# Order of long and short matmuls inside the products of an encoder layer's seven-product units

## The chip, the cores and the metric

The kernel runs on one core of a Trainium2 chip. The metric is device time in microseconds (us) of one execution. A core has a matrix engine (TensorE, here PE; the loading of its stationary operand is shown apart as PEld), a vector engine (VectorE, DVE), a scalar engine (ScalarE, ACT), a general one (GpSimd, POOL) and SyncE (SP), which here issues most of the DMA transfers. Each engine runs its own list of instructions in order, and semaphores tie the lists together. Working memory is SBUF; PE adds up its results in eight banks of PSUM.

## The reference

One encoder layer on 512 tokens of width 2048, in float32. Cut to what matters here:

```python
h = rmsnorm(x, attn_norm_w)
proj = h @ w_in                      # 2048 -> 6176 columns
attn_out = mixture_of_dilations(...) # 16 heads of 64, three windows
gla_out = ...                        # gated linear attention, both directions
x = x + concat(attn_out, gla_out) @ w_out
h = rmsnorm(x, ffn_norm_w)
x = x + (silu(h @ w_gate) * (h @ w_up)) @ w_down   # hidden width 5632
return rmsnorm(x, final_norm_w)
```

The matrix products with `w_in`, `w_gate`, `w_up` and `w_down` are most of the work.

## The kernel before, in words

Large products are computed in float32 accuracy from operands that are each split in a rounded part (`hi`) and the rest (`lo`). A product of two such numbers takes hi times hi, hi times lo and lo times hi; lo times lo is left out.

Part of the products with `w_in`, `w_gate` and `w_up` goes by a scheme that computes a two by two block product with seven block products instead of eight (Strassen's scheme in Winograd's form). The class `Units` does this. One *unit* is a block of 256 weight columns against all 512 tokens and the whole depth of 2048. It needs seven sums of weight blocks; each sum is a tile of 128 partitions by `NP` = 8 pieces of 128 columns. The sums of activations are made once and kept in `self.xs[q][name]`, one tile for each piece `q`, which holds 256 columns of hi next to 256 columns of lo.

One of the seven products (`products`) is sixteen matmuls into one PSUM bank. Eight **long** ones (512 moving columns, line 1669) multiply the eight pieces of the weights' hi tile with the activations' hi and lo together: hi times hi goes to the first half of the bank, hi times lo to the second. Eight **short** ones (256 moving columns, line 1672) multiply the eight pieces of the weights' lo tile with the activations' hi, and add to the first half. Every matmul loads another stationary operand of 128 by 128.

The tiles for product i are made in `lead(i)`, which is called two products ahead (`AHEAD` = 2): `cast` on ACT rounds the sum to hi (line 1631), `sub` on DVE subtracts it from the sum to get lo (line 1637), and `add` on DVE makes the next sum (line 1606) from weight blocks that SyncE loads (line 1599). After a product, `evac_` reads its bank with ACT and DVE. Where a later product of the unit adds to a result that is known already, `seat` first runs one long matmul on a fresh bank (line 1655) whose result is overwritten by that known value; it stands between two products.

Each engine's order is that of the program text. The hi and lo tiles come from one pool of `b` tiles (`s4`); `put(hi, lo)` gives them back after the product, and whoever writes such a tile next waits for its last reader.

Other streams of matmuls that the profile shows: lines 356 to 358 and 2118 to 2120 are long matmuls only (plain products and the one with `w_down`), lines 1768 to 1770 are short ones only (a unit in smaller pieces), and lines 731 and 732 are eight short ones in the attention, between transposes (line 707) and long ones.

Of the kernel before, what the change touches and what calls it, by code (L numbers as in the profile page):

```python
# [116 lines left out]
def put(*slots):  # L117
    for s in slots:
        if s.home is not None:
            s.home.free.append(s.i)  # L120


def layer(nc, tc, x, attn_norm_w, w_in, rel_table, gw_f, gb_f, gw_b, gb_b, gla_norm_w, w_out,
# [5 lines left out]
    mm = pe.matmul  # L129

    with tc.manual_schedule(), \
# [1190 lines left out]
        NP = KT // 2  # L1322
# [253 lines left out]
        class Units:  # L1576
# [82 lines left out]
            def products(self, i):  # L1659
                u, n = self.steps[i]  # L1660
                hi, lo = self.both.pop(i)
                k = "XVYXWZW"[n]
                new = n < 2
                if new:
                    b = self.banks[u, k] = ps.get()
                    ps.full.add(b.i)
                o = self.banks[u, k].t
                for q in range(NP):
                    mm(o.rearrange("p (s t) -> p s t", s=2), hi.t[:, q], self.xs[q][self.ORDER[n]],  # L1669
                       start=new and q == 0, stop=False, skip_group_check=True)  # L1670
                for q in range(NP):
                    mm(o[:, 0:256], lo.t[:, q], self.xs[q][self.ORDER[n]][:, 0], start=False, stop=q == NP - 1,  # L1672
                       skip_group_check=True)
                put(hi, lo)
                self.late_.append(i)

# [576 lines left out]
        def finish():  # L2253
# [43 lines left out]
            def last(ys):  # L2297
# [6 lines left out]
                for h in range(2):  # L2304
                    cols = slice(h * 256, (h + 1) * 256)
                    b = seeded.popleft()
                    products(b, t, c, cols)
                    dve.scalar_tensor_tensor(x_[:, cols], b.t[:, cols], rstd2[:, t:t + 1], x_[:, cols],
                                             op0=OP.mult, op1=OP.add)
                    put(b)  # L2310
                    if h == 0:
                        act.activation(junk.t[:, cols], x_[:, cols], AF.Square, accum_out=ss1[:, 3:4])
                        act.activation(ss1[:, 8:13], ss1[:, 0:5], AF.Copy, scale=1.0 / D, accum_out=total)
                        dve.tensor_tensor(ys[c].t[:, cols], x_[:, cols], wf[c].t[:, cols], op=OP.mult)
                        continue
                    dve.tensor_tensor_reduce(junk.t[:, cols], x_[:, cols], x_[:, cols], 1.0 / D, 0.0,
                                             op0=OP.mult, op1=OP.add, accum_out=sq)
                    act.activation(q, sq, AF.Ln, bias=total)
                    act.activation(r, q, AF.Exp, scale=-0.5)
                    dve.tensor_tensor(m, sq, total, op=OP.add)  # L2320
                    dve.tensor_tensor(ys[c].t[:, cols], x_[:, cols], wf[c].t[:, cols], op=OP.mult)
# [8 lines left out]
            def run():  # L2330
                ys = {t: [] for t in range(4)}
                behind = []

                def rest(t, c, b, y):
                    residual(c, t, b)
                    squares(c, t, x1[c], ss2 if t < 3 else ss1[:, 0:4], 0 if t == 3 else 4 * t)
                    if t == 3:
                        dve.tensor_tensor(y.t, x1[c][t].t, wf[c].t, op=OP.mult)
                    if c == 3:
                        later(t, ys[t])  # L2340
                        put(*ys[t], *(x1[c][t] for c in range(4)))

                for t, c in ORDER:
                    seed()
                    y = s2.get()
                    ys[t].append(y)
                    if (t, c) == (3, 3):
                        last(ys[t])
                        break
                    b = seeded.popleft()  # L2350
                    products(b, t, c, slice(0, 512))
                    behind.append((t, c, b, y))
                    while len(behind) > (t < 2):
                        rest(*behind.pop(0))
# [45 lines left out]
```

## Time and profile before

| what | value |
|---|---|
| three runs, median (lowest to highest) | 2131.49 us (2129.62 to 2131.94) |
| the profiled execution's own time | 2129.54 us |
| its span in the profile | 2127.3 us |
| granted TensorE clock, mean | 0.999 |
| long matmuls of the units (line 1669) | 3,248 |
| short matmuls of the units (line 1672) | 3,248 |
| seven-product units' products | 406 |

The profile comes from one execution. Its span runs from the first instruction of the program to the end of the last; the time of that execution is 2.2 us longer. "Busy" adds the recorded durations of an engine's instructions. In the timeline a row is a run of equal instructions: its first start, the time until its end, engine, line, operation, the tile written and those read, and how many. Matmuls overlap, and their ends are modelled, so a row's second number is longer than the time until the next row begins. In a view of one line, the durations of the instructions stand as lowest, median and highest in ns.

### The profile page before, as it was taken

The page shows a single profiled execution, that of the slowest core. Times are in us where ns is not written, and L with a number is a line of the kernel's source. Part 1 is how long each engine was busy: PE and PEld are TensorE (multiplying, and loading weights), DVE is VectorE, ACT ScalarE, POOL GpSimd, SP SyncE. Part 2 cuts the span into 40 slices and gives each one's busy share as a digit, 9 for nine tenths or more (in the row PEclk, how much of TensorE's full clock was granted, in tenths as well). Part 3 has the DMA queues.
Part 4 walks back from the last instruction along what each step waited for, and adds up shares of the span by engine and source line. Part 5 has one row for each costly group of instructions (what it writes and reads, how often), then busy time and mean ns, then how long its engine had stood idle before and what let it go on. Part 6 is the DMA issues. An engine that isn't in the chain of part 4 may idle for free.

```text
span 2127.3 us, 30896 instructions
## 1 busy us (share of the span) xinstructions
PE 2117.0 (100%) x11370; PEld 1822.8 (86%) x11370; DVE 1756.2 (83%) x2381; ACT 1281.3 (60%) x2152; POOL 205.5 (10%) x384
## 2 busy tenths in 40 slices
PE   9999999999999999999999999999999999999998
PEld 7888888888888889988888888888888888888886
DVE  6688888778877568888888999999999798876696
ACT  8454444468776556555555555555555477877774
POOL 0000000123222000000000011011011201111100
PEclk9999999999999999999999999999999999999999
DMA  6644544656664233444443445455455788975662
GB/s 206 177 130 129 139 139 135 181 156 194 195 177 122 98 119 100 139 123 125 120 128 113 151 145 172 139 165 158 142 166 157 276 292 297 332 243 184 228 218 80
DMA packets 342405, 355.65 MB, mean 167 GB/s; under 512 B 16686, under 2 KB 261918, under 8 KB 342255
## 3 DMA queue, kind: packets, MB, share of 16 engines
q1 hardware_dynamic: 310638, 251.78, 38.8%
q0 software_dynamic: 31296, 101.38, 13.6%
q8 instruction: 90, 1.47, 0.3%
q14 instruction: 61, 0.49, 0.1%
q10 hardware_dynamic: 320, 0.53, 0.1%
HBM read 289.57 MB, written 64.06 MB: 166 GB/s over the span
## 4 chain that ended last, share of the span: by engine, by line
PE 96%; DVE 2%; ACT 1%; issue 1%; DVEq 0%; ACTq 0%
PE ps L1669 35%; PE ps L1672 18%; PE ps L2120 6%; PE ps L2118 6%; PE ps L2119 6%; PE ps L358 5%; PE ps L356 5%; PE ps L357 5%; PE ps L707 1%; PE ps L732 1%; PE ps L651 1%; PE ps L731 1%; PE ps L652 1%; PE ps L1769 1%; PE ps L1768 1%
## 5 line engine op out<-in xcount | busy, mean ns | idle before, releaser
L1637 DVE TENSOR_TENSOR b<-b,b 128x1024 fp32r<-128x1024 f32 x406 | 495.7, 1221 | 73.4 <-ACT b L1631 71.3
L1631 ACT CAST b<-b 128x1024 fp32r<-128x1024 f32 x406 | 421.1, 1052 | 21.4 <-DMA b<-in_w_in_dram 15.1
L1669 PE MATMUL ps<-a,b 128*128 128x512 f32 x1656 | 424.5, 392 | 0.0
L1669 PE MATMUL ps<-b,b 128*128 128x512 f32 x1592 | 421.0, 393 | 0.0
L1669 PEld LDWEIGHTS ps<-a,b 128*128 128x128 f32 x1656 | 304.3, 188 | 62.6 <-ACT ps L1703 0.2
L1669 PEld LDWEIGHTS ps<-b,b 128*128 128x128 f32 x1592 | 280.2, 189 | 42.4
L1606 DVE TENSOR_TENSOR b<-b,b 128x1024 f32<-128x1024 f32 x232 | 282.6, 1218 | 12.8 <-DMA b<-in_w_in_dram 12.8
L1672 PEld LDWEIGHTS ps<-b,b 128*128 128x128 f32 x1592 | 232.6, 190 | 23.4
L1672 PE MATMUL ps<-b,b 128*128 128x256 f32 x1592 | 242.9, 282 | 0.0
L1672 PE MATMUL ps<-a,b 128*128 128x256 f32 x1656 | 242.6, 283 | 0.0
L1672 PEld LDWEIGHTS ps<-a,b 128*128 128x128 f32 x1656 | 224.7, 191 | 8.3
L2086 DVE TENSOR_TENSOR b<-b,b 128x1024 fp32r<-128x1024 f32 x140 | 170.7, 1221 | 69.4 <-ACT b L2078 66.3
L1697 ACT COPY b<-ps 128x256 f32<-128x256 f32 x126 | 46.9, 372 | 243.0 <-PE ps L1672 241.6
L2078 ACT CAST b<-b 128x1024 fp32r<-128x1024 f32 x140 | 146.4, 1049 | 17.0 <-DVE b L2066 7.2
L2118 PE MATMUL ps<-b,b 128*128 128x512 f32 x368 | 143.2, 389 | 0.0
L2119 PE MATMUL ps<-b,b 128*128 128x512 f32 x368 | 143.2, 389 | 0.0
L2120 PE MATMUL ps<-b,b 128*128 128x512 f32 x368 | 143.2, 389 | 0.0
L356 PE MATMUL ps<-b,b 128*128 128x512 f32 x256 | 104.7, 409 | 0.0
L358 PE MATMUL ps<-b,b 128*128 128x512 f32 x256 | 100.3, 392 | 0.1
L357 PE MATMUL ps<-b,b 128*128 128x512 f32 x256 | 100.0, 391 | 0.0
L2119 PEld LDWEIGHTS ps<-b,b 128*128 128x128 f32 x368 | 69.1, 188 | 14.4
L2120 PEld LDWEIGHTS ps<-b,b 128*128 128x128 f32 x368 | 69.1, 188 | 14.3
(307 smaller groups left out, 3610.7 us busy)
## 6 DMA issues: line engine op xcount, KB each, us to landing
b<-in_w_in_dram SPq DMA_DIRECT2D x94, 512.0 KB, 5.3
b<-in_w_gate_dram SPq DMA_DIRECT2D x88, 512.0 KB, 6.2
b<-in_w_up_dram SPq DMA_DIRECT2D x88, 512.0 KB, 4.5
b<-in_w_down_dram SPq DMA_DIRECT2D x88, 512.0 KB, 5.4
b<-gx POOLq DMA_DIRECT2D x46, 512.0 KB, 6.8
gx<-a POOLq DMA_DIRECT2D x84, 256.0 KB, 4.4
b<-in_w_out_dram SPq DMA_DIRECT2D x32, 512.0 KB, 4.3
a<-gx POOLq DMA_DIRECT2D x48, 256.0 KB, 6.0
```

The source lines that it names most:

```text
L356: mm(o, xh.t[:, c], wh.t[:, w], start=first and not on, stop=False, skip_group_check=on)
L357: mm(o, xh.t[:, c], wl.t[:, w], start=False, stop=False, skip_group_check=on)
L358: mm(o, xl.t[:, c], wh.t[:, w], start=False, stop=last, skip_group_check=on)
L1606: tt = lambda o, x_, y_: dve.tensor_tensor(o.t, x_.t, y_.t, op=OP.add)
L1631: act.copy(hi.t, home[key].t)
L1637: dve.tensor_tensor(lo.t, home[key].t, hi.f, op=OP.subtract)
L1669: mm(o.rearrange("p (s t) -> p s t", s=2), hi.t[:, q], self.xs[q][self.ORDER[n]], start=new and q == 0, stop=False, skip_group_check=True)
L1672: mm(o[:, 0:256], lo.t[:, q], self.xs[q][self.ORDER[n]][:, 0], start=False, stop=q == NP - 1, skip_group_check=True)
L2086: dve.tensor_tensor(lo.t, s.t, hi.f, op=OP.subtract)
L2118: mm(o, xh[:, t], wh, start=not ch and first and j == 0, stop=False, skip_group_check=True)
L2119: mm(o, xh[:, t], wl, start=False, stop=False, skip_group_check=True)
L2120: mm(o, xl[:, t], wh, start=False, stop=last and j == 1, skip_group_check=True)
```

## The change

Inside a product the sixteen matmuls are put in another order. Before, all eight long ones ran, then all eight short ones. Now the eight pieces go by pairs: for two pieces the long matmuls, then for the same two pieces the short ones, and so on four times. Each matmul has the operands and the bank that it had. The first of a product still opens the bank (`start`), and the last short one still closes it (`stop`).

```diff
-                for q in range(NP):
-                    mm(o.rearrange("p (s t) -> p s t", s=2), hi.t[:, q], self.xs[q][self.ORDER[n]],
-                       start=new and q == 0, stop=False, skip_group_check=True)
-                for q in range(NP):
-                    mm(o[:, 0:256], lo.t[:, q], self.xs[q][self.ORDER[n]][:, 0], start=False, stop=q == NP - 1,
-                       skip_group_check=True)
+                for p in range(0, NP, 2):
+                    for q in (p, p + 1):
+                        mm(o.rearrange("p (s t) -> p s t", s=2), hi.t[:, q], self.xs[q][self.ORDER[n]],
+                           start=new and q == 0, stop=False, skip_group_check=True)
+                    for q in (p, p + 1):
+                        mm(o[:, 0:256], lo.t[:, q], self.xs[q][self.ORDER[n]][:, 0], start=False, stop=q == NP - 1,
+                           skip_group_check=True)
```

The first place is on PE, in the third product of the kernel's first unit (the one that starts at 110.18 us in the trace before). A row gives the line, the tile written, the two read (activations, then the weights' hi or lo tile) and what the matmul waits for. Before (`b_109` is hi, `b_110` is lo):

```order
L1669 MATMUL ps_34_1105<-a_15_309,b_109_1084 128x512 [waits Activation_49]
L1669 MATMUL ps_34_1105<-a_23_382,b_109_1084 128x512
L1669 MATMUL ps_34_1105<-a_33_487,b_109_1084 128x512
L1669 MATMUL ps_34_1105<-a_41_608,b_109_1084 128x512
L1669 MATMUL ps_34_1105<-a_46_698,b_109_1084 128x512
L1669 MATMUL ps_34_1105<-a_50_799,b_109_1084 128x512
L1669 MATMUL ps_34_1105<-a_54_865,b_109_1084 128x512
L1669 MATMUL ps_34_1105<-a_58_929,b_109_1084 128x512
L1672 MATMUL ps_34_1105<-a_15_309,b_110_1086 128x256 [waits DVE_49]
L1672 MATMUL ps_34_1105<-a_23_382,b_110_1086 128x256
```

The same place on PE in the changed kernel, where the two lines are 1670 and 1673:

```order
L1670 MATMUL ps_34_1105<-a_15_309,b_109_1084 128x512 [waits Activation_49]
L1670 MATMUL ps_34_1105<-a_23_382,b_109_1084 128x512
L1673 MATMUL ps_34_1105<-a_15_309,b_110_1086 128x256 [waits DVE_49]
L1673 MATMUL ps_34_1105<-a_23_382,b_110_1086 128x256
L1670 MATMUL ps_34_1105<-a_33_487,b_109_1084 128x512
L1670 MATMUL ps_34_1105<-a_41_608,b_109_1084 128x512
L1673 MATMUL ps_34_1105<-a_33_487,b_110_1086 128x256
L1673 MATMUL ps_34_1105<-a_41_608,b_110_1086 128x256
L1670 MATMUL ps_34_1105<-a_46_698,b_109_1084 128x512
L1670 MATMUL ps_34_1105<-a_50_799,b_109_1084 128x512
```

The wait for DVE's lo moved from the ninth row of the product to the third, and the last reader of hi from the eighth to the fourteenth.

The second place is PE right behind this product: two seats (line 1655) and the head of the next product. Before:

```order
L1672 MATMUL ps_34_1105<-a_58_929,b_110_1086 128x256
L1655 MATMUL ps_36_1152<-b_8_164,b_111_1108 128x512 [waits PE_49,Activation_49]
L1655 MATMUL ps_37_1155<-b_8_164,b_111_1108 128x512 [waits PE_49]
L1669 MATMUL ps_33_1088<-b_12_190,b_111_1108 128x512
L1669 MATMUL ps_33_1088<-b_16_230,b_111_1108 128x512
L1669 MATMUL ps_33_1088<-b_26_299,b_111_1108 128x512
L1669 MATMUL ps_33_1088<-b_32_372,b_111_1108 128x512
```

And now:

```order
L1673 MATMUL ps_34_1105<-a_58_929,b_110_1086 128x256
L1655 MATMUL ps_36_1152<-b_8_164,b_111_1108 128x512 [waits PE_49,Activation_49]
L1655 MATMUL ps_37_1155<-b_8_164,b_111_1108 128x512 [waits PE_49]
L1670 MATMUL ps_33_1088<-b_12_190,b_111_1108 128x512
L1670 MATMUL ps_33_1088<-b_16_230,b_111_1108 128x512
L1673 MATMUL ps_33_1088<-b_12_190,b_112_1110 128x256 [waits DVE_49]
L1673 MATMUL ps_33_1088<-b_16_230,b_112_1110 128x256
```

The seats stay where they were, with the same waits; behind them four long matmuls in a row (two seats, two of the product) now stand ahead of the first short one, where there were ten. The orders of DVE, ACT, POOL and SyncE are those of before.

## The prediction

> **What bounds the kernel now.** I read the head of the page first, for the engine that sets the time.
>
> ```profile
> span 2127.3 us, 30896 instructions
> ...
> PE 2117.0 (100%) x11370; PEld 1822.8 (86%) x11370; DVE 1756.2 (83%) x2381; ACT 1281.3 (60%) x2152; POOL 205.5 (10%) x384
> ...
> PE 96%; DVE 2%; ACT 1%; issue 1%; DVEq 0%; ACTq 0%
> PE ps L1669 35%; PE ps L1672 18%; PE ps L2120 6%; PE ps L2118 6%; PE ps L2119 6%; PE ps L358 5%; PE ps L356 5%; PE ps L357 5%; PE ps L707 1%; PE ps L732 1%; PE ps L651 1%; PE ps L731 1%; PE ps L652 1%; PE ps L1769 1%; PE ps L1768 1%
> ```
>
> PE is busy for the whole span, and 96% of the chain that ended last is PE. Lines 1669 (long matmuls, 512 columns) and 1672 (short, 256 columns) hold 53% of the chain. The busy durations of matmuls overlap (a long one is shown at 389 ns), so the price of one is the distance from its start to the next start. Those distances come from the timeline: each row below is a run of matmuls with its first start, and the next row's start ends the run.
>
> ```profile
> 1002.14 0.52 PE L1672 MATMUL ps<-b,b 128*128 128x256 f32 x3
> 1002.49 0.76 PE L1672 MATMUL ps<-a,b 128*128 128x256 f32 x5
> 1003.09 2.00 PE L1669 MATMUL ps<-b,b 128*128 128x512 f32 x8
> 1004.93 1.11 PE L1672 MATMUL ps<-b,b 128*128 128x256 f32 x8
> 1005.88 0.86 PE L1669 MATMUL ps<-b,b 128*128 128x512 f32 x3
> 1006.58 1.31 PE L1669 MATMUL ps<-a,b 128*128 128x512 f32 x5
> 1007.72 0.52 PE L1672 MATMUL ps<-b,b 128*128 128x256 f32 x3
> ...
> 1195.83 0.86 PE L1669 MATMUL ps<-b,b 128*128 128x512 f32 x3
> ```
>
> Eight longs take 1.84 us and eight shorts 0.95 (of 2.793, below, I count 1841 and 952 ns). From 1003.09 to 1195.83 lie 69 products: 192.74 / 69 = 2.793 us each, with no gap between them. There are 406 products (3,248 = 1656 + 1592 longs, by eight), so 1134 us of the span goes by this price.
>
> **The price depends on place.** In the product at 1005.88 the first three longs take 0.70 us and the next five 1.14, that is 233 and 228 ns each. In the one that ends at 1003.09 the first three shorts take 0.35, the last five 0.60, 117 and 120 each. The 120 is the settled price of a short; that of a long is seen in a stream of nothing else:
>
> ```profile
> 1744.95 0.39 PE L2118 MATMUL ps<-b,b 128*128 128x512 f32 x1
> ...
> 1745.63 0.39 PE L2118 MATMUL ps<-b,b 128*128 128x512 f32 x1
> ```
>
> Three longs in 0.68 us are 227 ns each. A product at settled prices would be 8 x 347 = 2776 ns; it takes 2793. So going over from one width to the other costs 17 ns net in each product; there is one such round now, and there would be four. The recorded durations show the same places (the line's own view, over the first two longs, the fifth to eighth, and the eight shorts):
>
> ```profile
> L1669 PE MATMUL ps<-b,b x2: 396/396/397, 1003.1 to 1003.3; 128*128 128x512 f32 x2
> ...
> L1669 PE MATMUL ps<-b,b x4: 389/389/393, 1004.0 to 1004.7; 128*128 128x512 f32 x4
> ...
> L1672 PE MATMUL ps<-b,b x8: 278/283/283, 1004.9 to 1005.8; 128*128 128x256 f32 x8
> ```
>
> The first two longs behind shorts are 7 and 8 ns over the settled 389; the first short behind longs is 5 ns under the settled 283. That is a debit on two longs and a smaller refund on a short. The rest of the debit, 1841 - 8 x 227 - 15 = 10 ns, lies on the third to eighth long, which a pair never reaches.
>
> **The change part by part.** No matmul is added or removed; each of the 406 products becomes four groups of long, long, short, short. *The pair of longs behind shorts*: lines 1655 and 1669 show such a pair (two seats, behind the eight shorts of the product at 110.18).
>
> ```profile
> 110.18 2.11 PE L1669 MATMUL ps<-a,b 128*128 128x512 f32 x8
> 112.13 1.12 PE L1672 MATMUL ps<-a,b 128*128 128x256 f32 x8
> 113.08 0.63 PE L1655 MATMUL ps<-b,b 128*128 128x512 f32 x2
> 113.55 1.99 PE L1669 MATMUL ps<-b,b 128*128 128x512 f32 x8
> ```
>
> The pair takes 0.47 us. From 0.70 for three, less 228 for the third, it is 472; from the durations, 2 x 227 + 15 = 469. I take 469, since the starts are rounded to 10 ns. *The pair of shorts behind longs*: 0.95 for eight less six settled ones (720) is 230; from the durations, 240 less 5 and 1 is 234. I take 232. A group is then 701 ns, a product 4 x 701 = 2804 against 2793: 11 ns x 406 = **+4.5 us**. What is unknown is whether a pair of shorts suffices to bring about the debit, and whether longs that are not settled still give the refund. Neither stands anywhere in the trace, so I bound it: below by settled longs with the refund, 2 x 227 + 232 = 686 (product 2744, -49 ns, -20 us); above by the debit without the refund, 469 + 240 = 709 (2836, +43 ns, +17.5 us). The value taken lies near the middle of these, and is the only one of which both halves are rows of this very loop.
>
> *The wait for lo.* The first short waits for DVE's lo (L1637). It now stands third, 0.47 us into the product where it stood 1.84 us in, and thirteen matmuls are queued behind it. The margins:
>
> ```profile
> 109.96 1.23 DVE L1637 TENSOR_TENSOR b<-b,b 128x1024 fp32r<-128x1024 f32 x1 [1.37 <-DMA vd<-b]
> 112.92 1.23 DVE L1637 TENSOR_TENSOR b<-b,b 128x1024 fp32r<-128x1024 f32 x1 [1.73 <-ACT b L1631]
> ...
> 1193.61 1.22 DVE L1637 TENSOR_TENSOR b<-b,b 128x1024 fp32r<-128x1024 f32 x1
> ```
>
> The lo of the product at 110.18 is ready at 111.19; its first short, due at about 110.65, waits 0.54 us. The next product's lo comes at 114.15 and would be due at 113.55 + 0.47, but it is already 0.54 later by then, so that wait is no second one. In the steady part the tightest product is that of 1195.83, whose lo is ready at 1194.83, 1.0 us ahead of its first long. So this term is **+0.5 us**; without that cover each product would lose what lo is late.
>
> *Release of hi.* The last reader of a hi tile is now the fourteenth matmul, not the eighth: about 0.7 us later. Its slot goes to later loads and casts.
>
> ```profile
> SPq L1599 <- PE ps L1669: 51.8, 20, 3.4
> ```
>
> SyncE waits for L1669 before 20 loads (the queue's own waits: total, times, longest), so 20 loads may start 0.7 us later. The groups of the two lines that read or follow such loads:
>
> ```profile
> L1631 ACT CAST b<-b 128x1024 fp32r<-128x1024 f32 x406 | 421.1, 1052 | 21.4 <-DMA b<-in_w_in_dram 15.1 <-DVE b L1606 3.1 <-DVE b L1637 2.3
> ...
> L1606 DVE TENSOR_TENSOR b<-b,b 128x1024 f32<-128x1024 f32 x232 | 282.6, 1218 | 12.8 <-DMA b<-in_w_in_dram 12.8
> ```
>
> DVE and ACT waited for loads only 12.8 and 15.1 us in all, and ACT's casts never for PE, so I cost it at nothing: the loads' lead hides it. Were that cover gone for all 20, it would be 14 us. DVE's and ACT's own orders stay as they were.
>
> The sum, against the profiled execution's 2129.54 us (span 2127.3 and 2.2 around it): 2129.5 + 4.5 + 0.5 = **2134.5 us**. The median of the three runs before is 2131.49, 2.0 above this execution.
>
> **The rivals.** *The pair settles at once* (faster). Behind shorts that were not in the settled 120, the second long came at the settled price:
>
> ```profile
> 551.45 0.28 PE L732 MATMUL ps<-b,b 128*128 128x256 f32 x1
> 551.56 0.40 PE L356 MATMUL ps<-b,b 128*128 128x512 f32 x1
> 551.80 0.39 PE L357 MATMUL ps<-b,b 128*128 128x512 f32 x1
> 552.02 0.39 PE L358 MATMUL ps<-b,b 128*128 128x512 f32 x1
> ```
>
> Two longs in 0.46 us: a group is 462 + 232 = 694, a product 2776, -17 ns, -6.9 us: 2123. For it: two shorts alone may leave PE in such a state. Against it: in the loop itself, the second short is within 1 ns of the settled duration.
>
> *No refund* (slower). The refund is what settled longs hand to the first short; longs still paying the debit hand on nothing. Group 709, +17.5 us: 2147.5. It is slower than now from a group of 698 (2793 / 4) up.
>
> *Loads run further ahead* (much faster). Each weight load is on record at the start of the matmul ahead of it, here the first long's behind L732's matmul:
>
> ```profile
> 551.45 0.19 PEld L356 LDWEIGHTS ps<-b,b 128*128 128x128 f32 x1
> ```
>
> If shorts are held at 120 by their loads, and the spare time in longs could take two loads, the shorts would go at the refund's price, 232 - 120 = 112 each: 8 x (227 + 112) = 2712, -81 ns, -33 us: 2097. The rows speak against it: L356's load starts with L732's matmul at 551.45, one matmul ahead and no more. The Trainium skill, "TensorE: Matmul & The Clock Gate", section "The mechanism", holds that loads overlap matmuls in flight only for another row group; the trace does not agree, since here full 128-row loads lie inside matmuls. The same page's table at its head has a 64-deep queue that pulls loads ahead of matmuls in flight, which would speak for this rival.
>
> *The order is free.* If the 17 ns are owed to something once in a product (its boundary) and not to the changes of width, nothing but lo's 0.5 us remains: 2130. Against it: the extra lies behind the shorts also where seats, not the product, come first (113.08). The Trainium skill, the same page, section "Back-to-back issue gap", gives a warm gap of N / 2.4 + 2.5 ns whatever went before; by it a product would be 8 x (215.8 + 109.2) = 2600 ns in either order. The trace shows 2793 and a price that depends on place, so the measurement decides against it.
>
> **How the numbers follow.** The forecast, that rows of now repeat four times, has 0.42; the pair settles 0.25; no refund 0.18; order free 0.10; loads further ahead 0.05. About 0.2% (4.3 us) is what a measurement of this kernel can tell from no change, and the forecast's +5.0 stands on that bound: half of it counts as same, a little below. Faster: 0.25 + 0.05 + 0.02 = 0.32. Same: 0.10 + 0.18 = 0.28. Slower: 0.18 + 0.22 = 0.40. The range, 2118 to 2145, holds the forecast, the settled pair and the free order, with part of the way to either bound (2110 and 2147.5).
>
> **What would show it.** Four steps of 0.70 us in a product's timeline confirm the forecast; long durations of 396 and 397 with first shorts of 278 the two halves of it. Durations of 389 in each second long show the settled pair, shorts of 283 throughout show no refund, and loads that start ahead of the matmul before show the third rival. A gap on PE at 110.7 of 0.5 us shows the wait for lo; waits of PE for DVE at other products, or of DVE for DMA in the later stages, would make the prediction wrong by something I costed at nothing.

## The result and the profile after

| kernel | median of runs (lowest to highest) | ratio to the kernel before, 95% interval |
|---|---|---|
| before | 2130.91 us (2129.55 to 2132.66), 22 runs | |
| changed | 2127.58 us (2127.30 to 2128.21), 22 runs | 0.9985 (0.9978 to 0.9992) |

The kernel became faster by 0.15%. That is less than the 0.2% which the prediction took as the least that can be told from no change, but the interval of the ratio leaves 1 out. The forecast was 2134.5, slower than the profiled execution by 0.23%.

The head of the page and the chain that ended last, of the changed kernel:

```profile
span 2126.0 us, 30896 instructions
...
PE 2114.2 (99%) x11370; PEld 1811.3 (85%) x11370; DVE 1756.4 (83%) x2381; ACT 1281.5 (60%) x2152; POOL 205.5 (10%) x384
...
PE 96%; DVE 2%; ACT 1%; issue 1%; DMA 0%; POOL 0%; SPq 0%; DVEq 0%; ACTq 0%; POOLq 0%
```

PE bounds it as before. The timeline of PE over half a product (two rounds of long, long, short, short) and the start of the next round, where line 1670 is the long matmul and 1673 the short one:

```profile
1003.51 0.62 PE L1670 MATMUL ps<-b,b 128*128 128x512 f32 x2
1003.97 0.40 PE L1673 MATMUL ps<-b,b 128*128 128x256 f32 x2
1004.21 0.63 PE L1670 MATMUL ps<-b,b 128*128 128x512 f32 x2
1004.68 0.39 PE L1673 MATMUL ps<-b,b 128*128 128x256 f32 x2
1004.90 0.62 PE L1670 MATMUL ps<-b,b 128*128 128x512 f32 x2
```

Two kinds of round alternate. In the first the longs take 0.46 us and the shorts 0.24, in the second 0.47 and 0.22. The starts in the trace are whole ns; their mean distances over some 395 undisturbed products of each kernel (ns, first matmul to last) are

```
before   233.3 235.8 228.3 232.5 230.9 226.7 226.7 226.7   113.3 119.2 120 120 120 120 120 120    sum 2793.3
changed  232.5 230.9 113.3 119.2   233.3 235.9 115.8 112.5   (twice)                              sum 2786.7
```

The sums are those of the means before rounding. So a product lost 6.7 ns. That gives 2.7 us over the 406 products, of which 0.7 went again to waits for lo. From the first long of the first product to the start of the last short, the kernel before took 1588.73 us and the changed one 1586.69. These 2.04 us are what the profiles show of the change; the lowest runs of the two differ by 2.25. The rest of the 3.3 us between the medians lies elsewhere and is taken up below, with the second and third profile of the kernel before (1588.58 and 1588.76 us over the same stretch).

### The profile page after: what moved, and what is told of

Same layout as the page of the kernel before. It is cut to its first block, busy times and chain, and to the rows that moved or that the text cites. A ratio compares the mean times of both kernels' runs of the same rounds, so it can differ in the third digit from the quotient of the medians.

```text
span 2126.0 us, 30896 instructions
## 1 busy us (share of the span) xinstructions
PE 2114.2 (99%) x11370; PEld 1811.3 (85%) x11370; DVE 1756.4 (83%) x2381; ACT 1281.5 (60%) x2152; POOL 205.5 (10%) x384
## 4 chain that ended last, share of the span: by engine, by line
PE 96%; DVE 2%; ACT 1%; issue 1%; DMA 0%; POOL 0%; SPq 0%; DVEq 0%; ACTq 0%; POOLq 0%
PE ps L1670 35%; PE ps L1673 18%; PE ps L2119 6%; PE ps L2120 6%; PE ps L2121 6%; PE ps L358 5%; PE ps L356 5%; PE ps L357 5%; PE ps L707 1%; PE ps L731 1%; PE ps L651 1%; PE ps L732 1%; PE ps L652 1%; PE ps L1770 1%; PE ps L1769 1%
## 5 line engine op out<-in xcount | busy, mean ns | idle before, releaser
L1670 PE MATMUL ps<-a,b 128*128 128x512 f32 x1656 | 536.7, 396 | 0.0
L1670 PE MATMUL ps<-b,b 128*128 128x512 f32 x1592 | 515.9, 395 | 0.0
L1673 PEld LDWEIGHTS ps<-a,b 128*128 128x128 f32 x1656 | 311.0, 188 | 74.7 <-DVE b L1637 0.8
L1673 PEld LDWEIGHTS ps<-b,b 128*128 128x128 f32 x1592 | 299.0, 188 | 70.4 <-DVE b L1637 0.3
L1673 PE MATMUL ps<-a,b 128*128 128x256 f32 x1656 | 341.1, 278 | 0.3 <-DVE b L1637 0.3
L1673 PE MATMUL ps<-b,b 128*128 128x256 f32 x1592 | 329.4, 278 | 0.0
L1670 PEld LDWEIGHTS ps<-a,b 128*128 128x128 f32 x1656 | 259.9, 189 | 0.3 <-ACT ps L1704 0.2
L1670 PEld LDWEIGHTS ps<-b,b 128*128 128x128 f32 x1592 | 249.2, 188 | 0.3
L2120 PE MATMUL ps<-b,b 128*128 128x512 f32 x368 | 143.2, 389 | 0.0
L2119 PE MATMUL ps<-b,b 128*128 128x512 f32 x368 | 143.2, 389 | 0.0
L2121 PE MATMUL ps<-b,b 128*128 128x512 f32 x368 | 143.2, 389 | 0.0
L356 PE MATMUL ps<-b,b 128*128 128x512 f32 x256 | 104.6, 409 | 0.8 <-DVE b L487 0.8
L358 PE MATMUL ps<-b,b 128*128 128x512 f32 x256 | 100.3, 392 | 0.2 <-DVE b L474 0.2
L357 PE MATMUL ps<-b,b 128*128 128x512 f32 x256 | 100.1, 391 | 0.2 <-DVE b L488 0.2
L2121 PEld LDWEIGHTS ps<-b,b 128*128 128x128 f32 x368 | 69.1, 188 | 14.5
L2119 PEld LDWEIGHTS ps<-b,b 128*128 128x128 f32 x368 | 69.1, 188 | 14.3
```

What stands on the lines that cost most here:

```text
L356: mm(o, xh.t[:, c], wh.t[:, w], start=first and not on, stop=False, skip_group_check=on)
L357: mm(o, xh.t[:, c], wl.t[:, w], start=False, stop=False, skip_group_check=on)
L358: mm(o, xl.t[:, c], wh.t[:, w], start=False, stop=last, skip_group_check=on)
L2119: mm(o, xh[:, t], wh, start=not ch and first and j == 0, stop=False, skip_group_check=True)
L2120: mm(o, xh[:, t], wl, start=False, stop=False, skip_group_check=True)
L2121: mm(o, xl[:, t], wh, start=False, stop=last and j == 1, skip_group_check=True)
```

## The experiments

The ratios are to runs of the kernel before that were taken beside each group of experiments. Their median was 2130.28 us beside the first four; 2130.75 beside the two-six order with the old start and the cut short, on another chip; and 2130.05 beside the pairs, on the first chip again. Medians of different groups are compared with this in mind.

The unit of the expectations is 0.833 ns, because in it all the means above are whole numbers within 0.03: 280, 283, 274, 279, 277, 272 for longs, 136, 143, 144, 139, 135 for shorts. A product of before is then 3352 units, one of the changed kernel 3344, both multiples of 8. Eight units, 6.67 ns, are the *grid step*, and a matmul's *place* is its start modulo 8 units, counted from the first long behind settled shorts. Following the places through both kernels, equal place, width and width before had equal prices: for instance a long behind a long at place 4 costs 277 in both, as fifth long before and as second long now. That became the theory to test (the *theory of the grid* in the expectations), against a price that belongs to the place in the run of equal widths (their *price by place*).

### Two rounds, of two and of six

```diff
-                for q in range(NP):
-                    mm(o.rearrange("p (s t) -> p s t", s=2), hi.t[:, q], ...)
-                for q in range(NP):
-                    mm(o[:, 0:256], lo.t[:, q], ...)
+                l = s = 0
+                for kind in "LLssLLLLLLssssss":
+                    if kind == "L":
+                        mm(o.rearrange("p (s t) -> p s t", s=2), hi.t[:, l], ...)
+                        l += 1
+                    else:
+                        mm(o[:, 0:256], lo.t[:, s], ...)
+                        s += 1
```

> Every product runs long, long, short, short, six long, six short. Theory of the grid: what a matmul costs depends on its width, on the width before it, and on where its start falls in a grid of 6.67 ns; the starts of before and after give these costs as 280, 283, 274, 279, 277, 272 (long) and 136, 143, 144, 139, 135 (short) units of 0.833 ns, and followed step by step from the start behind settled shorts this order costs 280 283 139 135 279 277 272 272 272 272 136 143 144 144 144 144, together 3336 units or 2780 ns a product: 7 ns under the changed kernel, 13 under the one before, about 5.4 us off the kernel before (near 2125.5). Rival, price by place in the run: the first round costs as measured in the changed kernel (697 ns), the second as the first six longs and six shorts of the kernel before (2099 ns), together 2796: 9 ns over the changed kernel, 1 us over the one before (near 2132).

It took 2125.35 us, ratio 0.9976 (0.9967 to 0.9985). A product costs 2780 ns, the figure that the theory of the grid gave, and the units are those written down, in order. The timeline, with this kernel's lines 1671 (long) and 1675 (short):

```profile
1002.82 0.63 PE L1671 MATMUL ps<-b,b 128*128 128x512 f32 x2
1003.29 0.39 PE L1675 MATMUL ps<-b,b 128*128 128x256 f32 x2
1003.51 1.53 PE L1671 MATMUL ps<-b,b 128*128 128x512 f32 x6
1004.88 0.88 PE L1675 MATMUL ps<-b,b 128*128 128x256 f32 x6
1005.60 0.63 PE L1671 MATMUL ps<-b,b 128*128 128x512 f32 x2
```

The six longs take 1.37 us; replayed from the head of the old run they would take 1.387. The rival's 2796 is 16 ns off, so the price does not belong to the place in the run. The stretch from the first long to the last short is 1584.22 us, 4.5 under the kernel before and not 5.4, because the first products of each run of units lose about 0.9 us, most of it to late lo.

### One and one

In the same loop the order is `"Ls" * 8`.

> Every product runs long, short in turn, eight times. Theory of the grid: a pair comes to a whole number of grid steps once it repeats, so a product costs 2773, 2800 or 2827 ns (pairs of 346.7, 350 on average, or 353.3); which of them it cannot say, since a short behind a long at 0 in the grid after only one long has not been seen. Price by place: 233 + 113 = 346 a pair, 2768. Loads run further ahead than one matmul: 227 + 113 = 340, 2720, 30 us off the kernel before.

The median was 2128.19 us, but the twelve runs fell in three groups: 2122.9 to 2123.4 (five), 2128.2 to 2129.8 (five), 2143.3 and 2143.9; the ratio is 0.9992 (0.9972 to 1.0012). The profiled execution is one at 2143.89 and holds two prices by itself: ten products cost 2772 to 2780 ns, 389 cost 2815 to 2835. The durations of the longs and of the shorts that read an `a` tile, in a stretch of the first kind (117 to 127 us):

```profile
L1671 PE MATMUL ps<-a,b x15: 392/392/395, 117.6 to 125.5; 128*128 128x512 f32 x15
...
L1675 PE MATMUL ps<-a,b x15: 274/274/280, 117.8 to 125.8; 128*128 128x256 f32 x15
```

and of the second kind (1000 to 1100 us):

```profile
L1671 PE MATMUL ps<-a,b x143: 395/398/403, 999.7 to 1099.4; 128*128 128x512 f32 x143
...
L1675 PE MATMUL ps<-a,b x143: 277/281/284, 1000.0 to 1099.6; 128*128 128x256 f32 x143
```

The same order on the same engine has two prices, 277 135 279 141 units in one stretch and 289 144 283 136 279 141 in the other, according to how PE came into it: the ten products stand in two stretches, each behind a product that waited for lo (at 110.6 and 881.4 us), and each stretch ends at a seat (at 128.65 and 898.82 us). A price by width and neighbours cannot do this. Had the 389 products cost 2773 too, the execution would have been 20.8 us shorter, 2123.1, which is where the first group lies; no run of that group or of the middle one was profiled. Both repeat in a whole number of grid steps (104 and 159). The theory could not say which of them would come, as it had stated. Loads that run further ahead (2720) are out: in both patterns a short right behind a long costs up to 120, and the longs cost 230.8 or more.

### Four and four

The order is `"LLLLssss" * 2`.

> Every product runs four long, four short, twice. Price by place: 233+236+228+232 and 113+119+120+120, 1401 a half, 2802 a product: 3.6 us over the kernel before. A fixed price for each change of width (2.8 ns a round, as in the changed kernel): 2782. Theory of the grid: the longs cost 280 283 274 279 units (930 ns), the shorts behind them start at a place not seen before, and the half comes to a multiple of 6.67 ns: 1393 (2787), 1400 (2800) or 1407 (2813).

2135.21 us, ratio 1.0023 (1.0014 to 1.0032): slower. A product costs 2806.7 ns, and no line of the expectation has it: the replay is 5 ns under, the fixed price 25, and the nearest values of the theory, 2800 and 2813, are 7 off. The two halves differ (282 280 283 269 141 144 144 144, then 280 283 274 279 141 143 141 140 units), and only the two together are a whole number of steps, 421. It shows that the theory is not complete either. Followed by its places, a long behind a long at place 3 costs 274 in one half and 280 in the other; so PE carries more than the place and the last width. The theory can therefore be trusted along steps that have been seen, with what led up to them, and not beyond.

### The third product in the old order

In the changed kernel, the order is that of before where `i == 2`.

> The changed kernel, but the third product of each run of units keeps the old order (eight long, eight short): the one at 111 us whose first short waits for lo, and the one at 877 us. If that wait is what the change costs there, the product at 111 us shrinks by 0.5 us and the one at 877 by 0.1, and the kernel comes out 0.6 us under the changed one (near 2127.0). Rival: the wait only moves to the next product, whose lo comes late too: no difference.

2127.47 us, against 2127.58 for the changed kernel: no difference. The timeline at that place, PE:

```profile
110.33 2.11 PE L1671 MATMUL ps<-a,b 128*128 128x512 f32 x8
112.29 1.11 PE L1675 MATMUL ps<-a,b 128*128 128x256 f32 x8
113.24 0.63 PE L1655 MATMUL ps<-b,b 128*128 128x512 f32 x2
113.70 0.62 PE L1671 MATMUL ps<-b,b 128*128 128x512 f32 x2
114.37 0.50 PE L1675 MATMUL ps<-b,b 128*128 128x256 f32 x2
114.71 0.63 PE L1671 MATMUL ps<-b,b 128*128 128x512 f32 x2
```

The third product, at 110.33, no longer waits. The fourth, at 113.70, does: its two longs and two shorts take 0.67 and 0.34 us instead of 0.47 and 0.23. The rival was right; the lo of two products in a row comes late, and the long run ahead of the shorts had covered both.

### Two and six, with the old order in the third and the fourth

Two-six order, but eight and eight where `i in (2, 3)`.

> Every product runs long, long, short, short, six long, six short, but the third and the fourth of each run of units keep eight long, eight short. If the waits for lo at 111 and 114 us are what those two products lost (the old order in the third alone only moved the wait to the fourth), both go and the kernel comes out 0.5 to 0.8 us under the same order without this exception (2125.35): near 2124.7. Rival: the later products there are held by DVE in any order; no difference.

2124.37 us, ratio 0.9972 (0.9961 to 0.9983), the lowest median of this study. It is 1.0 us under two-six alone, but the two were taken on different chips; in their profiles the stretch from the first long to the last short is 0.8 us shorter (1583.46 against 1584.22), within what was forecast. No product waits for lo at the start any more.

### A short cut by eight columns

The order is that of before; the last short of each product has 248 columns:

```diff
                 for q in range(NP):
-                    mm(o[:, 0:256], lo.t[:, q], self.xs[q][self.ORDER[n]][:, 0], ...)
+                    w = 248 if q == NP - 1 else 256
+                    mm(o[:, 0:w], lo.t[:, q], self.xs[q][self.ORDER[n]][:, 0, 0:w], ...)
```

> The order of the kernel before, but the last short of each product has 248 columns instead of 256 (eight columns of the lo part are left out in one of eight pieces), which is 3.3 ns less of work. Price by place or by width alone: every product 3.3 ns shorter, 2790, 1.35 us in all. Theory of the grid: the next longs start half a grid step off, cost other amounts, and the product comes to a whole number of steps of 6.67 ns: 2787, 2793 or 2800, or a mean between these over a few products, but not 3.3 ns less in each; and the longs behind the cut short are no longer 233, 236, 228, 232, 231.

2124.84 us, ratio 0.9974 (0.9965 to 0.9984). Timeline of PE, longs 1669 and shorts 1673:

```profile
1003.76 0.86 PE L1669 MATMUL ps<-b,b 128*128 128x512 f32 x3
1004.46 1.30 PE L1669 MATMUL ps<-a,b 128*128 128x512 f32 x5
1005.59 0.52 PE L1673 MATMUL ps<-b,b 128*128 128x256 f32 x3
1005.94 0.76 PE L1673 MATMUL ps<-a,b 128*128 128x256 f32 x5
1006.54 1.99 PE L1669 MATMUL ps<-a,b 128*128 128x512 f32 x8
```

From 1003.76 to 1006.54 a product takes 2.78 us, in the trace 2780 ns: 13.3 less than before, two grid steps, where 3.3 ns of work were taken out. The cut short itself costs 140 units instead of 144. The longs behind it start at place 4 and cost 281 279 277 272 272 instead of 280 283 274 279 277: they are settled two matmuls sooner. The list of results that I gave was too short (2780 is not on it), and the price of the first long, 281, had not been seen before. But the next ones, 279, 277 and 272, are those that a long behind a long has at these places in the kernel before, and neither a price by place in the run nor one by width gives any gain in longs that were not touched.

### Pairs of products

Where `n` is 0, 3 or 5, and at `i == 2`, the order is eight and eight; elsewhere, where `n` is 2, 4 or 6, it is `"ssssssLLssLLLLLL"`; else two-six.

> Of a unit's seven products the third, fifth and seventh run six short, long, long, short, short, six long; the product behind each of these (fourth, sixth, and the next unit's first) runs eight long, eight short, so that fourteen longs stand in a row; the second runs long, long, short, short, six long, six short; the first unit's third and fourth keep the old order. Theory of the grid, step by step: 720 + 697.5 + 1370 = 2787 for a product of the first kind (behind settled shorts), 2766 for the one behind it (all its longs settled at 227), 2780 for the second: 5553 a pair against 5560 for two products of two-six. Three pairs in each of 58 units save 1.2 us against the two-six order with the old start (2124.37): near 2123.2. Rival: what is saved at one change of width comes back at the next, or lo, now wanted at the start of three products in seven, is late: 2124.4 or more.

2124.87 us, ratio 0.9976 (0.9966 to 0.9985): half a microsecond over the two-six order with the old start, which was taken on another chip. The products cost 2787, 2766 and 2780 ns, each as written down, and first long to last short is 0.9 us shorter (1582.6 against 1583.5). It is lost again behind the last unit, at the first wait on PE there:

```profile
1702.12 0.50 PE L2123 MATMUL ps<-b,a 128*128 128x512 f32 x1 [0.54 <-DVE b L2090]
```

From the last short to the end of the span are 435.3 us, against 434.3 in the order it is compared with. The products were priced right, and the kernel still did not gain, because PE came to the next stage before DVE had its operand. DVE itself had waited 4.5 us there for a load of the gated values, and started on it 10.9 us behind the last short, where it was 9.5. Whether the order or chance made the load later, one profile of each does not show.

### The kernel before, twice more

> The kernel before once more, for a second and a third profile of it: its times spread over 3 us, those of the changed kernel over 1 us. If the spread lies in the products (another state of the same order), some products cost other than 2793 ns in a slower execution; if it lies in the start (loads before the first product at 104 us), the products agree and their first one starts later.

> As the run before it: where a slower execution of the unchanged kernel spends its extra time, in the products or ahead of the first one.

They took 2129.31 and 2131.03 us. The 406 products sum to 1134.3 us in both, as in the first profile, so the spread is not there. The first product starts at 104.24 and 104.99 us (and at 105.02 in the profile of the changed kernel, 104.19 in that of before). The slower one also waits behind the last unit, where the product with `w_down` begins. PE, and DVE ahead of it, in that execution:

```profile
1707.49 0.39 PE L2118 MATMUL ps<-b,a 128*128 128x512 f32 x1
1708.19 0.50 PE L2119 MATMUL ps<-b,a 128*128 128x512 f32 x1 [0.30 <-DVE b L2086]
...
1704.30 0.43 DVE L1335 TENSOR_TENSOR a<-b 128x256 f32<-128x256 f32 x1 [4.25 <-DMA b<-gd]
```

The step from 1707.49 to 1708.19 is 0.47 us over the settled 0.23, two more steps there add 0.1 each. DVE had waited 4.25 us for a load of the gated values. So the 1.7 us between the two profiles are the start, 0.75 us, this seam, about 0.75, and 0.2 in between. In the profile of the changed kernel the seam holds no such wait, and DVE waits less ahead of it:

```profile
DVE a L1335 <- DMA b<-gd: 1.8, 1, 1.8
```

That this accounts for the 1.3 us between the 3.3 of the medians and the 2.04 of the profiles is likely. DVE started on that load 9.2, 10.0 and 10.6 us behind the last short in the three profiles of the kernel before, and PE lost nothing, 0.1 and 0.7 us; it was 8.1 in the changed kernel and 8.4 in the run with the old third, and PE lost nothing. But these are few executions, and what would make the load land sooner is not shown. Whether the change shortens that wait, or the executions only happened so, stays open.

## Why the prediction was wrong

**What bounds the kernel: right.** PE without gaps, 53% of the chain in the two lines, and a price that depends on the order of the matmuls. The order is not free: the same sixteen matmuls cost from 2766 to 2835 ns in these runs, according to order and to what went before. The Trainium skill, "TensorE: Matmul & The Clock Gate", section "Back-to-back issue gap", gives N / 2.4 + 2.5 ns for an isolated warm matmul, and about 131 ns at 512 columns for a stream of loads and matmuls; the 2600 ns of the prediction is an estimate by the first of these. Neither is seen here: at a granted clock of 0.999 the settled price of 512 columns is 226.7 ns.

**The term that failed: a group at 701 ns.** I took the pair of longs at 469 (the debit of the first two of a run of eight) and the pair of shorts at 232 (the refund of the first two), and repeated both four times: 2804. The two doubts named there were the right ones, "whether a pair of shorts suffices to bring about the debit, and whether longs that are not settled still give the refund", and neither held in the form taken. Measured: in every second round the longs pay 469.2, as taken, and the shorts behind them 228.3, a larger refund than 232; in the rounds between, the shorts pay 232.5, as taken, and the longs only 463.4. The rounds are 697.5 and 695.9, the mean 696.7, 4 ns under what was taken, and 698.3 was the point where gain turns to loss. The term is -2.7 us in place of +4.5. The forecast lay 2.7 ns a round above that point and the measurement 1.6 below it, so that what I had named as confirming the forecast, four steps of 0.70 us, could not tell them apart: 697.5 and 695.9 ns are 0.70 too.

The mistake beneath it is that I took prices that pass with the state of PE for a fixed toll on each change of width. The prices at the head of the old run were taken as belonging to "first and second long behind shorts". They belong to where PE stands when the run begins, and a run of two leaves it elsewhere than a run of eight. The cut short shows it best: 3.3 ns less of work ahead of a run of longs makes that run 10 ns cheaper. How far the place in the grid alone describes that state is open, as the four-four order shows. The durations that I quoted (396 and 397 for the first two longs) were true, and no row of the trace before had a run of two to read the rest from.

**The rivals.** The settled pair (694 a group) came nearest: 695.9 in every second round, though by a cheaper first and second long together and not by a second long at 227. No refund: out, with shorts of 278 and less:

```profile
L1670 PE MATMUL ps<-b,b x8: 393/396/397, 1003.5 to 1005.8; 128*128 128x512 f32 x8
...
L1673 PE MATMUL ps<-b,b x6: 274/278/283, 1004.0 to 1005.5; 128*128 128x256 f32 x6
```

These are the durations of the eight longs and the first six shorts of one product of the changed kernel. The first shorts are at 277 or 278 in every round (but for the two that waited for lo), and every second pair has its second one at 274, below any short of the old loop; that is the larger refund. Loads further ahead and the free order are out by the runs.

**The wait for lo: right in place, nearly in size.** PE and DVE of the changed kernel:

```profile
111.01 0.73 PE L1670 MATMUL ps<-a,b 128*128 128x512 f32 x2
112.09 0.50 PE L1673 MATMUL ps<-a,b 128*128 128x256 f32 x2 [0.34 <-DVE b L1637]
...
110.81 1.23 DVE L1637 TENSOR_TENSOR b<-b,b 128x1024 fp32r<-128x1024 f32 x1 [1.39 <-DMA vd<-b]
```

That product took 3508 ns where it took 2903: +0.6 for the +0.5 of the sum. The product at 877 us, which I had not listed, lost 0.1. That the next product needs no second wait, because it comes later by the first one, held too: the run with the old third takes the first wait away, and the second appears.

**The release of hi: right, nothing.** SyncE waited longer for PE before its loads (364.5 us for line 1673, where lines 1672 and 1669 had 300.6 and 51.8), but the loads' lead hid it. DVE's and ACT's groups, whose waits for loads are as before:

```profile
L1631 ACT CAST b<-b 128x1024 fp32r<-128x1024 f32 x406 | 420.1, 1048 | 20.6 <-DMA b<-in_w_in_dram 15.1 <-DVE b L1606 2.8 <-DVE b L1637 2.0
...
L1606 DVE TENSOR_TENSOR b<-b,b 128x1024 f32<-128x1024 f32 x232 | 282.8, 1219 | 12.7 <-DMA b<-in_w_in_dram 12.7
```

## What to carry to other kernels

On a PE that hardly waits, the price of a matmul in a mixed stream of widths was not a property of the matmul in these runs: compare orders by the time of a whole repeating pattern on the chip, and do not build a new order from the heads of old runs. An order that returns PE to the same point in each product (two-six here) took 2125.1 to 2125.9 us in nine runs, while one that does not (one-one) gave the fastest and the slowest executions of all, 2122.9 and 2143.9, in twelve. Where a gain of a few ns repeats hundreds of times, look at the seams: a wait there for another engine can give it back.

## What the runs showed of the hardware that was not expected

- Mean distances between matmul starts are whole multiples of 0.833 ns, within 0.03 of a unit in the kernel before, the changed one and four-four; the whole ns of the trace blur them by up to 0.4 in the others. Every order that settled repeats in a multiple of 6.67 ns: products of 3352, 3344, 3336 and 3368 units, and two cycles of one-one of 832 and 1272. After uniform widths PE falls into 226.7 ns for 512 columns and 120.0 for 256, and needs up to five matmuls behind a change of width to get there in the old loop.
- Taking eight columns out of one matmul in sixteen took 13.3 ns out of the product, 3.3 of them in that matmul.
- What the grid is in the hardware was not settled. Each matmul has a weight load beside it in all these orders, and no run separated the two.
